# Spreading the per-token norms of the next block over the partitions: four matmuls with a broadcast column, in place of a VectorE product with the identity and one matmul with ones

## The chip, the cores and the metric

The kernel runs on one core of a Trainium2 chip. The metric is the device time of one execution in microseconds (us); of the kernel before, three runs have a median of 1286.19 us (1285.68 to 1287.00).

## The reference, cut to what matters

One layer of a streaming encoder is computed for 2048 new frames (with 16 meta tokens ahead of them) and for 32 frames of a running stream. The sums of the attention, the short convolution and the output projection stand in the kernel too; only the lines around the change are shown.

```python
def rmsnorm(x, g):
    xf = x.astype(f32)
    y = xf * lax.rsqrt(jnp.mean(xf * xf, axis=-1, keepdims=True) + EPS)
    return (y * g.astype(f32)).astype(x.dtype)
...
    q, k, v, z_a, b_g, c_g, u, z_c = split_proj(rmsnorm(hp, norm_g[l]), w_in[l])   # 1024 -> 4096 columns
...
    # attention per head: softmax(q1 k1 / 8 + bias) - lambda * softmax(q2 k2 / 8 + bias), times v
    # beside it: gated causal convolution of width 3; both are concatenated, projected, added to x, normed
```

The kernel projects x times g without its norm, and multiplies the norm of each token (one number, rsqrt of its mean square) into the results. In the projection's results the tokens lie along the free axis, so the 512 norms of a block must stand on all 128 partitions: that is the tile `rb`.

## The kernel before, in words

The 2048 frames are worked in four blocks of 512 tokens (`p` = 0 to 3; the first one carries the 16 meta tokens and the 32 sample frames as well). Within a block there are four head units `unit_a(h, p)`: projections of q, k, v and the gate z, each 24 matmuls of 512 columns (8 slices of the contraction, each as three products of high and low fp32r parts: `xh*wh`, `xl*wh`, `xh*wl`, line 225). `attend(h, p)` follows: score matmuls (L446, L447) into three buffers `s`, a minimum per row (L393, L396), an exponential (L397) which frees the score buffer, the coefficients (L370 to L377), scaling on ScalarE (L400) and combining on VectorE (L401), transposes (L462) and products with v (L469 to L471). `unit_c` computes the convolution. At the end the output projection runs in two halves (L693).

The values of v take a detour: VectorE multiplies the projection by the norms into `g` (L305), four transposes on TensorE (`ptv`, L316) turn it, and everything TensorE has behind them in its queue waits for them.

The next block is prepared during the last heads of a block. `x_stats(p + 1)` loads its rows in eight pieces `xr` (256 KB each), ScalarE squares and sums them (L115), and a short chain on VectorE and ScalarE (L117, L178 to L184) makes `r`, four norms on each partition: column t of `r` holds the norms of the 128 tokens of tile t. `x_rms(p + 1, r)` spreads `r`: VectorE multiplies the identity by each column of `r` into `dg` (four diagonal matrices side by side, L127), one fp32 matmul with `ones` as weights sums over the partitions into `pb` (L129), and ScalarE copies `pb` to `rb` (L130). `x_load(p + 1)` then loads the transposed tokens in eight pieces `xt` and splits each into `xh` (ScalarE, L152) and `xl` (VectorE, L153).

The pieces `xr`, `xt` and the product `dg` come out of one pool with the tag `xt` and eight buffers (XB = 8). `dg` is written as soon as `r` is there and is read by the matmul at the block's end, so one of the eight buffers is held for that long. Every tile of the tags `x0` to `x3` (`r` among them) and `rb` has one buffer; `pb` uses one of the two PSUM buffers `pj` of the projections.

No order is written out by hand: a scheduler puts the instructions of each engine into an order by its own estimate of time, `high_priority` moves some ahead, and each engine's queue then runs strictly in that order, SyncE's DMA issues included. So a small edit can move instructions on all engines. The transfers of weights (`wr`, 512 KB, from line 198), the loads of `xr` and `xt` and all stores are issued from SyncE's queue (the helper of line 80).

Of the kernel before, what the change touches and what calls it, by code (L numbers as in the profile page):

```python
# [11 lines left out]
F32 = mybir.dt.float32  # L12
F32R = mybir.dt.float32r
AF = mybir.ActivationFunctionType
ALU = mybir.AluOpType
AX = mybir.AxisListType

P = 128
# [9 lines left out]
QT = 512  # L28
# [7 lines left out]
XB = 8  # L36
# [11 lines left out]
def hybrid_step(ctx: ExitStack, tc: tile.TileContext, x, xT, ckT, cv, scT, rel_bias, norm_g, w_in,  # L48
# [10 lines left out]
    op = pool("op", 3)  # L59
    ap = pool("ap", 2)  # L60
    sm = pool("sm", 3)
    one = pool("one", 1)
# [6 lines left out]
    V, S, G, T = nc.vector, nc.scalar, nc.gpsimd, nc.tensor  # L69
# [16 lines left out]
    ident = const.tile([P, P], F32, name="ident")  # L86
    make_identity(nc, ident)
    ones = const.tile([P, P], F32, name="ones")
# [19 lines left out]
    def x_stats(p):  # L108

        ssq = sm.tile([P, 8], F32, tag="ssq", name="ssq", bufs=1)  # L110
        for j in range(8):
            xr = one.tile([P, QT], F32, tag="xt", name="xr", bufs=XB)
            r0 = NX + QT * p + P * (j // 2)
            dma(xr, x[r0:r0 + P, 512 * (j % 2):512 * (j % 2) + 512])
            S.activation(xr, xr, AF.Square, accum_out=ssq[:, j:j + 1])  # L115
        ssp, var, r, w = (sm.tile([P, 4], F32, tag=f"x{i}", name=f"x{i}", bufs=1) for i in range(4))
        V.tensor_reduce(ssp, ssq.rearrange("p (t i) -> p t i", i=2), op=ALU.add, axis=AX.X)  # L117
        rsqrt(r, ssp, var, w, 1.0 / D)
        return r

    def x_rms(p, r):

        rb = one.tile([P, NX + QT], F32, tag="rb", name="rb")
        pb = ps_j.tile([P, 512], F32, tag="pj", name="pb")
        dg = one.tile([P, QT], F32, tag="xt", name="dg", bufs=XB)
        with tc.high_priority():
            V.tensor_tensor(by_tile(dg), ident.unsqueeze(1).broadcast_to([P, 4, P]),  # L127
                            r.unsqueeze(2).broadcast_to([P, 4, P]), op=ALU.mult)
            T.matmul(pb, lhsT=ones, rhs=dg, start=True, stop=True)  # L129
            S.copy(rb[:, :QT], pb)  # L130
        rbs[p] = rb

# [101 lines left out]
    by_tile = lambda a: a.rearrange("p (t c) -> p t c", c=P)  # L234
# [512 lines left out]
    for p in range(NQ):  # L747
        for h in range(H):
            bz = one.tile([P, 512], F32, tag="bz", name="bz", bufs=2)
            if (h, p) != (0, 0):  # L750
                dma(bz, bzd[h])
            st = unit_a(h, p)
            if h == 2 and p < NQ - 1:
                r = x_stats(p + 1)
            if (h, p) == (0, 0):
                dma(bz, bzd[h])
            st["bz"] = bz
            if h == H - 1 and p < NQ - 1:
                x_rms(p + 1, r)
                x_load(p + 1)  # L760
            attend(h, p, st)
            if p == 0:
                attend_sample(h, st)
            for u in after[p == NQ - 1][h]:
                unit_c(u, p)
# [53 lines left out]
```

## Time and profile before

| what | value |
|---|---|
| runs, median of 3 | 1286.19 us (1285.68 to 1287.00) |
| the profiled execution's own time | 1287.04 us |
| its span | 1285.3 us |
| TensorE (PE) matmul busy | 1264.1 us, 98% of the span |
| weight loads (PEld) busy | 1099.2 us, 86% |
| VectorE (DVE) / ScalarE (ACT) / GpSimd (POOL) busy | 921.1 / 827.9 / 699.6 us |
| mean granted TensorE clock | 0.996 |

How to read it: PE, PEld, DVE, ACT, POOL and SP (SPq for its queue) are the engines; a row names the line, the operation, what it writes and reads, and in brackets how long the engine sat idle before it and what ended that. Two matmuls overlap in time, so the useful number for TensorE is the distance from start to start. L12 is line 12 of the kernel. An fp32 matmul stands as two records (two weight loads, two passes), an fp32r one as one.

### The profile page before, as it was taken

How to read it: one execution, taken by the hardware profiler on the slowest of the kernel's cores; microseconds unless marked ns; L12 is line 12 of the kernel's file. 1: busy time of each engine (PE TensorE's matmuls, PEld its weight loads, DVE VectorE, ACT ScalarE, POOL GpSimd, SP SyncE). 2: the span in 40 equal slices, each digit the busy share in tenths (PEclk: the TensorE clock that was granted, in tenths of full speed). 3: DMA queues.
4: the chain of work that ended last, by engine and by line, in shares of the span. 5: the costliest groups of instructions: out<-in, count | busy, mean ns of one | idle time of the engine just before them, and what ended most of it. 6: DMA issues, size and time to landing. Idle time of an engine off the chain costs nothing.

```text
span 1285.3 us, 21646 instructions
## 1 busy us (share of the span) xinstructions
PE 1264.1 (98%) x7058; PEld 1099.2 (86%) x7058; DVE 921.1 (72%) x2086; ACT 827.9 (64%) x2030; POOL 699.6 (54%) x918
## 2 busy tenths in 40 slices
PE   7999999999999998999999999999999999999997
PEld 6999999988888886888888888888888888888875
DVE  8667566567786847787878667767786896766663
ACT  6745454675776647677767567777777787764331
POOL 5775857767556675455465556454656483443300
PEclk9999999999999999999999999999999999999999
DMA  9744444675435447544353453344335443557752
GB/s 286 231 117 129 141 115 117 209 241 153 133 114 159 139 127 225 168 137 148 99 172 112 144 181 112 126 149 116 108 99 164 164 118 129 189 157 250 231 201 75
DMA packets 108048, 198.74 MB, mean 155 GB/s; under 512 B 17408, under 2 KB 45600, under 8 KB 107936
## 3 DMA queue, kind: packets, MB, share of 16 engines
q1 hardware_dynamic: 107936, 197.37, 49.4%
q8 instruction: 55, 0.90, 0.3%
q14 instruction: 57, 0.47, 0.1%
HBM read 145.62 MB, written 43.26 MB: 147 GB/s over the span
## 4 chain that ended last, share of the span: by engine, by line
PE 59%; DVE 1%; ACT 1%; DMA 0%; issue 0%; DVEq 0%; ACTq 0%
PE pj L225 27%; PE po L693 14%; PE s L446 4%; PE s L447 4%; PE pt L462 4%; PE po L469 2%; PE po L471 2%; PE po L470 2%; PE po L685 1%; DMA xr<-in_x 0%; PE ptv L316 0%; PE pm L474 0%; DVE p L401 0%; ACT p L397 0%; PE pss L423 0%; PE pss L424 0%
## 5 line engine op out<-in xcount | busy, mean ns | idle before, releaser
L78 POOL TENSOR_TENSOR wl<-wr,wh 128x256 fp32r<-128x256 f32 x480 | 376.8, 808 | 302.7 <-ACT wh L204 281.5
L225 PE MATMUL pj<-xh,wh 128*128 128x512 f32 (+2 forms) x1280 | 456.7, 358 | 3.2 <-DVE g L352 1.2
L225 PE MATMUL pj<-xl,wh 128*128 128x512 f32 (+2 forms) x1280 | 452.9, 354 | 1.8 <-DVE xl L153 1.8
L225 PE MATMUL pj<-xh,wl 128*128 128x512 f32 (+2 forms) x1280 | 452.4, 354 | 0.0
L225 PEld LDWEIGHTS pj<-xh,wh 128*128 128x128 f32 x1280 | 242.0, 189 | 35.2 <-issue 2.2
L225 PEld LDWEIGHTS pj<-xl,wh 128*128 128x128 f32 x1280 | 242.0, 189 | 30.7 <-DVE xl L153 2.6
L225 PEld LDWEIGHTS pj<-xh,wl 128*128 128x128 f32 x1280 | 241.6, 189 | 29.9 <-issue 0.2
L397 ACT ACTIVATE p<-s,nm 128x384 f32<-128x384 f32 (+5 forms) x352 | 208.3, 594 | 68.9 <-DVE nm L396 41.8
L204 ACT CAST wh<-wr 128x512 fp32r<-128x512 f32 x256 | 157.4, 618 | 102.5 <-PE pj L225 71.3
L401 DVE SCALAR_TENSOR_TENSOR p<-p,cf,p 128x384 f32<-128x384 f32 (+5 forms) x176 | 126.4, 747 | 24.2 <-ACT p L400 24.0
L396 DVE TENSOR_REDUCE nm<-s 128x1 f32<-128x384 f32 (+3 forms) x224 | 122.6, 560 | 22.8 <-PE s L447 22.5
L466 DVE TENSOR_TENSOR al<-pt,ah 128x512 fp32r<-128x512 f32 x144 | 97.1, 684 | 48.2 <-ACT ah L465 47.8
L78 POOL TENSOR_TENSOR cll<-ct,chh 128x256 fp32r<-128x256 f32 x80 | 64.9, 833 | 118.3 <-ACT chh L671 118.1
L446 PE MATMUL s<-ks,q 128*128 128x384 f32 (+5 forms) x352 | 127.3, 363 | 0.9 <-ACT p L397 0.8
L447 PE MATMUL s<-ks,q 128*128 128x384 f32 (+5 forms) x352 | 122.5, 349 | 0.0
L400 ACT ACTIVATE p<-p,cf 128x384 f32<-128x384 f32 (+5 forms) x176 | 99.1, 623 | 28.3 <-DVE cf L377 25.6
L465 ACT CAST ah<-pt 128x512 fp32r<-128x512 f32 x144 | 81.2, 585 | 43.0 <-PE pt L462 42.0
L393 DVE CUSTOM_DVE_ANT_0 s<-s,bz 128x512 f32<-128x512 f32 (+5 forms) x128 | 74.6, 588 | 22.0 <-PE s L447 19.7
L462 PE MATMUL pt<-ident,p 128*128 128x128 f32 x544 | 86.0, 272 | 0.0
L470 PE MATMUL po<-al,vh 128*128 128x256 f32 x288 | 82.5, 286 | 0.0
L469 PE MATMUL po<-ah,vh 128*128 128x256 f32 x288 | 81.7, 284 | 0.0
L471 PE MATMUL po<-ah,vl 128*128 128x256 f32 x288 | 81.2, 282 | 0.0
(237 smaller groups left out, 2185.4 us busy)
## 6 DMA issues: line engine op xcount, KB each, us to landing
wr<-in_w_in SPq DMA_DIRECT2D x128, 512.0 KB, 3.7
ct<-cat SPq DMA_DIRECT2D x28, 512.0 KB, 4.7
q<-q SPq DMA_DIRECT2D x64, 128.0 KB, 3.0
out<-y SPq DMA_DIRECT2D x32, 256.0 KB, 3.6
ks<-ksd SPq DMA_DIRECT2D x8, 776.0 KB, 5.0
xr<-in_x SPq DMA_DIRECT2D x24, 256.0 KB, 4.6
out<-g SPq DMA_DIRECT2D x24, 256.0 KB, 3.1
xt<-in_xT SPq DMA_DIRECT2D x24, 256.0 KB, 5.2
```

Source lines behind the costliest of these rows:

```text
L78: (engine or G).tensor_tensor(out[:, c0:c1], a[:, c0:c1], b[:, c0:c1], op=op)
L204: S.copy(wh, wi)
L225: T.matmul(ps, lhsT=a[:, k % 4], rhs=b[k][:, b0:b1], start=(k == 0 and i == 0), stop=(k == KT - 1 and i == 2))
L396: V.tensor_reduce(nm[:, c, j:j + 1], s, op=ALU.min, axis=AX.X)
L397: S.activation(pr[j][c], s, AF.Exp, bias=nm[:, c, j:j + 1], scale=-1.0, accum_out=l[:, c, j:j + 1])
L401: V.scalar_tensor_tensor(a0, a1, cf[:, 1, j:j + 1], a0, op0=ALU.mult, op1=ALU.add)
L446: T.matmul(ps, lhsT=qd[c][0][:, qs], rhs=ks[c][:, col:col + w], start=True, stop=False)
L447: T.matmul(ps, lhsT=qd[c][1][:, qs], rhs=ks[c][:, col:col + w], start=False, stop=True)
L462: T.transpose(pt[:, i, P * qi:P * (qi + 1)], cols(aa[qi], NM + P * (2 * j + i), P), ident)
L469: T.matmul(po, lhsT=vh[:, kt], rhs=ah[:, i], start=(kt == 0), stop=False)
L470: T.matmul(po, lhsT=vh[:, kt], rhs=al[:, i], start=False, stop=False)
L693: T.matmul(ps, lhsT=a[k][:, :rows], rhs=b[k], start=(k == 0 and i == 0), stop=(k == KT - 1 and i == 2))
```

## The change

The product with the identity and its buffer `dg` go. The matmul with ones becomes four matmuls of 128 columns: the weights are column t of `r`, repeated 128 times by a stride of zero, the moving operand is the identity. Each writes its quarter of `pb`.

```diff
         rb = one.tile([P, NX + QT], F32, tag="rb", name="rb")
         pb = ps_j.tile([P, 512], F32, tag="pj", name="pb")
-        dg = one.tile([P, QT], F32, tag="xt", name="dg", bufs=XB)
         with tc.high_priority():
-            V.tensor_tensor(by_tile(dg), ident.unsqueeze(1).broadcast_to([P, 4, P]),
-                            r.unsqueeze(2).broadcast_to([P, 4, P]), op=ALU.mult)
-            T.matmul(pb, lhsT=ones, rhs=dg, start=True, stop=True)
+            for t in range(4):
+                T.matmul(pb[:, P * t:P * (t + 1)], lhsT=r[:, t:t + 1].broadcast_to([P, P]), rhs=ident,
+                         start=True, stop=True)
             S.copy(rb[:, :QT], pb)
         rbs[p] = rb
```

The scheduler answers the edit with another order in many places. Three of them matter below; all lie around the end of block 1, when block 2 is loaded and the statistics of block 3 are made. Lines of the changed kernel from 129 on are one lower than in the kernel before (L305 is L304, L393 is L392, L397 is L396, L401 is L400, L446 is L445), and the numbers behind names differ by a few.

The first is VectorE's queue around the evacuation of v (L305, `g_6971`, or `g_6973` in the change), which the transposes `ptv` wait for. `cf` are the coefficients of the softmax, `s_6701` and `s_6706` (`s_6703`, `s_6708`) two score tiles of 512 columns. Before:

```order
L184 TENSOR_TENSOR x2_8734<-x2_8734,x3_8735 128x4
L376 TENSOR_TENSOR r2_6616<-r2_6616,lam2_141 128x2
L127 TENSOR_TENSOR dg_9741<-ident_100,x2_8734 128x512
L377 TENSOR_TENSOR cf_6615<-nm_6589,r2_6616 128x2x2
L393 ISA s_6701,nm_6685<-s_6701,bz_6285 128x512
L393 ISA nm_6685 128x1
L305 TENSOR_TENSOR g_6971<-pj_6984,rb_6492 128x512
```

and in the change:

```order
L183 TENSOR_TENSOR x2_8736<-x2_8736,x3_8737 128x4
L375 TENSOR_TENSOR r2_6618<-r2_6618,lam2_141 128x2
L376 TENSOR_TENSOR cf_6617<-nm_6591,r2_6618 128x2x2
L392 ISA s_6703,nm_6687<-s_6703,bz_6286 128x512
L392 ISA nm_6687 128x1
L392 ISA s_6708,nm_6687<-s_6708,bz_6286 128x512
L400 SCALAR_TENSOR_TENSOR p0_6593<-p1_6594,cf_6617,p0_6593 128x400
L400 SCALAR_TENSOR_TENSOR p0_6605<-p1_6606,cf_6617,p0_6605 128x384
L369 TENSOR_REDUCE M2_6715<-nm_6687 128x2
L304 TENSOR_TENSOR g_6973<-pj_6986,rb_6493 128x512
```

The product is gone from the queue, and a second score tile, two combining steps and a small reduction now stand ahead of the evacuation.

The second is TensorE's queue at the same place. Before:

```order
L447 MATMUL s_6706<-ks1_6342,q11_6291 128x512
L446 MATMUL s_6730<-ks0_6341,q00_6288 128x272
L447 MATMUL s_6730<-ks0_6341,q01_6289 128x272
L316 MATMUL ptv_7014<-ident_100,g_6971 128x128 x4
L225 MATMUL pj_7039<-xh0_6500,wh_7031 128x512
L225 MATMUL pj_7039<-xl0_6501,wh_7031 128x512
```

and in the change:

```order
L445 MATMUL s_6732<-ks0_6342,q00_6289 128x272
L446 MATMUL s_6732<-ks0_6342,q01_6290 128x272
L445 MATMUL s_6737<-ks1_6343,q10_6291 128x272
L446 MATMUL s_6737<-ks1_6343,q11_6292 128x272
L461 MATMUL pt_6633<-ident_100,p0_6593 128x128
...
L461 MATMUL pt_6648<-ident_100,p0_6605 128x128
L445 MATMUL s_6744<-ks0_6342,q00_6289 128x384
L446 MATMUL s_6744<-ks0_6342,q01_6290 128x384
L315 MATMUL ptv_7016<-ident_100,g_6973 128x128 x4
L224 MATMUL pj_7041<-xh0_6502,wh_7033 128x512
```

Two more pairs of score matmuls and six transposes now stand ahead of `ptv`; before, they came after it.

The third is SyncE's queue, from the last piece of block 2 to the weights of the next head (`wr_7508`, or `wr_7510` in the change). Before:

```order
L80 DMA xt_6540<-in_xT 128x512
L80 DMA vd3_135<-vl_6432 128x512
L80 DMA xr_8708<-in_x 128x512
...
L80 DMA xr_8729<-in_x 128x512
L80 DMA wr_7508<-in_w_in 128x1024
L80 DMA q00_6869<-q00_6869 64x512
```

and in the change:

```order
L80 DMA xr_8710<-in_x 128x512
L80 DMA vd3_135<-vl_6433 128x512
L80 DMA xr_8713<-in_x 128x512
...
L80 DMA xr_8731<-in_x 128x512
L80 DMA xt_9748<-in_xT 128x512
...
L80 DMA xt_9790<-in_xT 128x512
L80 DMA wr_7510<-in_w_in 128x1024
L80 DMA q00_6871<-q00_6871 64x512
```

The last piece `xt` of block 2 went far ahead, the first `xr` of block 3 has its place, and all eight `xt` of block 3 (2 MB) now stand ahead of the weights.

## Rows read from the trace of the kernel before

**Rows 1.** The page's busy times: engine, us (share of the span), instructions.

```profile
PE 1264.1 (98%) x7058; PEld 1099.2 (86%) x7058; DVE 921.1 (72%) x2086; ACT 827.9 (64%) x2030; POOL 699.6 (54%) x918
```

**Rows 2.** Who TensorE waited for, over the whole span: us in total, times, longest.

```profile
PE pv L601 <- DMA oh<-in_ohd: 3.9, 1, 3.9
PE ptv L316 <- DVE g L305: 3.4, 2, 3.2
PE pj L225 <- DVE xl L153: 1.8, 3, 1.2
PE pj L225 <- DVE g L352: 1.2, 2, 1.0
PE s L446 <- ACT p L397: 0.8, 1, 0.8
```

**Rows 3.** The tiles `pb` and `dg`: engine, line, operation, count, duration in ns (min/median/max), first and last start in us.

```profile
L129 PE MATMUL pb<-dg,ones x6: 591/592/592, 249.8 to 762.4; 128*128 128x512 f32 x6
L127 DVE TENSOR_TENSOR dg<-ident,x x3: 694/1175/1191, 59.0 to 511.9; 128x512 f32<-128x512 f32 x3
```

**Rows 4.** Weight loads in order of time, around `pb` of block 1: start us, us, row, count.

```profile
249.63 0.31 PEld L129 LDWEIGHTS pb<-dg,ones 128*128 128x128 f32 x2
250.18 0.19 PEld L446 LDWEIGHTS s<-ks,q 128*128 128x128 f32 x1 [0.24 <-issue]
250.61 0.19 PEld L447 LDWEIGHTS s<-ks,q 128*128 128x128 f32 x1 [0.24 <-issue]
```

**Rows 5.** Matmuls in order of time, around the sample's product with v, an fp32 matmul of 64 columns with 128 columns of weights (eight records in a row): start us, us, row, count.

```profile
94.53 1.00 PE L518 MATMUL pos<-o,cvt 128*128 128x64 f32 x8
95.46 0.43 PE L518 MATMUL pos<-o,cvn 48*128 48x64 f32 x2
```

**Rows 6.** TensorE in order of time, from 509.9 us on (block 1, third head).

```profile
511.21 0.40 PE L446 MATMUL s<-ks,q 128*128 128x272 f32 x1 [0.78 <-ACT p L397]
511.45 0.28 PE L447 MATMUL s<-ks,q 128*128 128x272 f32 x1
514.90 1.11 PE L316 MATMUL ptv<-ident,g 128*128 128x128 f32 x4 [3.17 <-DVE g L305]
516.24 0.63 PE L225 MATMUL pj<-xl,wh 128*128 128x512 f32 x1
516.67 0.63 PE L225 MATMUL pj<-xh,wl 128*128 128x512 f32 x1
...
520.06 0.39 PE L225 MATMUL pj<-xl,wh 128*128 128x512 f32 x1
520.29 0.39 PE L225 MATMUL pj<-xh,wl 128*128 128x512 f32 x1
...
522.14 0.82 PE L462 MATMUL pt<-ident,p 128*128 128x128 f32 x6
522.72 0.37 PE L446 MATMUL s<-ks,q 128*128 128x272 f32 x1
...
523.05 0.34 PE L446 MATMUL s<-ks,q 128*128 128x384 f32 x1
523.22 0.34 PE L447 MATMUL s<-ks,q 128*128 128x384 f32 x1
```

**Rows 7.** Stretches of the same place: from:to, length, busy us (instructions) of PE, PEld, DVE, ACT, POOL, granted TensorE clock, DMA share, GB/s.

```profile
511.30:513.20 1.90, 0.43 (x2) 0.21 (x2) 1.90 (x4) 0.00 (x0) 1.82 (x3) 1.00 0.87 240
513.20:520.00 6.80, 5.10 (x14) 4.22 (x15) 4.72 (x16) 4.15 (x11) 2.83 (x4) 0.50 1.05 363
520.00:524.00 4.00, 4.00 (x24) 3.46 (x23) 2.32 (x4) 2.96 (x6) 1.76 (x2) 1.00 0.47 182
```

**Rows 8.** VectorE in order of time: the product of block 2 at 276 us, and the place at 511 us.

```profile
276.06 1.19 DVE L127 TENSOR_TENSOR dg<-ident,x 128x512 f32<-128x512 f32 x1
...
511.86 1.18 DVE L127 TENSOR_TENSOR dg<-ident,x 128x512 f32<-128x512 f32 x1
512.96 0.68 DVE L377 TENSOR_TENSOR cf<-nm,r 128x4 f32<-128x4 f32 x1
513.56 0.69 DVE L393 CUSTOM_DVE_ANT_0 s<-s,bz 128x512 f32<-128x512 f32 x1
514.16 0.68 DVE L305 TENSOR_TENSOR g<-pj,rb 128x512 f32<-128x512 f32 x1
514.77 0.62 DVE L401 SCALAR_TENSOR_TENSOR p<-p,cf,p 128x400 f32<-128x400 f32 x1
515.31 0.69 DVE L393 CUSTOM_DVE_ANT_0 s<-s,bz 128x512 f32<-128x512 f32 x1
```

**Rows 9.** ScalarE in order of time at the same place.

```profile
509.97 0.60 ACT L204 CAST wh<-wr 128x512 fp32r<-128x512 f32 x1
...
513.67 1.13 ACT L400 ACTIVATE p<-p,cf 128x400 f32<-128x400 f32 x2 [2.51 <-DVE cf L377]
514.71 0.60 ACT L204 CAST wh<-wr 128x512 fp32r<-128x512 f32 x1
515.22 0.68 ACT L397 ACTIVATE p<-s,nm 128x512 f32<-128x512 f32 x1
```

**Rows 10.** ScalarE in order of time: the first writing of `r` for block 2 (270.86, line 179), the last piece of block 2 and the first square for block 3, and the last such square (501.79).

```profile
270.86 0.21 ACT L179 ACTIVATE x<-x 128x4 f32<-128x4 f32 x1
...
488.69 0.61 ACT L204 CAST wh<-wr 128x512 fp32r<-128x512 f32 x1
492.82 0.72 ACT L152 ACTIVATE xh<-xt,ng 128x512 fp32r<-128x512 f32 x1 [3.51 <-DMA xt<-in_xT]
494.17 0.63 ACT L115 ACTIVATE xr<-xr 128x512 f32<-128x512 f32 x1 [0.63 <-DMA xr<-in_x]
...
501.79 0.64 ACT L115 ACTIVATE xr<-xr 128x512 f32<-128x512 f32 x1
```

**Rows 11.** SyncE's DMA issues in order of time: start us, us of issuing, row, count.

```profile
486.44 0.44 SPq L80 DMA_DIRECT2D xt<-in_xT  x1
...
487.81 7.44 SPq L80 DMA_DIRECT2D xr<-in_x  x7
...
505.31 0.33 SPq L80 DMA_DIRECT2D wr<-in_w_in  x1
505.73 1.88 SPq L80 DMA_DIRECT2D q<-q  x3
```

## The prediction

> **What bounds the kernel now.** I read the page's busy times first, then TensorE's waits, then the stretches in which they lie. TensorE is the bound: matmuls cover 98% of the span, VectorE only 72% [rows 1]. The five longest waits of TensorE come to 11 us, and half of that (3.9 and 1.8) is the loading at the start [rows 2]. So an edit on VectorE gives nothing in itself; what counts is TensorE's own work and the few places where its queue stands still. The worst is at 511 us: TensorE idles 0.78 us and then 3.17 us, until VectorE's evacuation of v (L305) lets `ptv` start at 514.90 [rows 6]. [...] There a 512-column matmul starts 0.43 us after the one before (516.24 to 516.67), against 0.23 us from 520 us on (520.06 to 520.29) [rows 6]; the 5.1 us of work done there [rows 7] would have taken half, so the low clock costs 2.5 us. Idling and clock are 3.95 + 2.5 = 6.5 us, the most that can be won at one place. One of the three products `dg` lies just there, at 511.86 [rows 8].
>
> **Part 1, TensorE's own work.** Before: `pb` is two passes of 512 columns. Its neighbours' weight loads start 0.43 us apart (250.18, 250.61) [rows 4], which is the length of a pass; two are 0.86 us a block. After: four fp32 matmuls, eight loads and eight passes of 128 columns. No row has this shape. Streaming alone gives 0.43/4 = 0.107 us a pass, 0.86 us in all: the lower bound, so no gain. The nearest row is the sample's product: also 128 columns of weights to load, 64 to stream, eight records from 94.53 to 95.46, 0.116 us each [rows 5]. There the load sets the pace, not the half as long streaming. At that pace eight passes take 0.93 us, 0.07 more than before; for three blocks **+0.2 us**, all of it on the path, since TensorE is the bound. I take this value. The upper bound adds a load that nothing covers, 0.107 us for each of 24 passes: +2.6 us.
>
> The rows argue against that upper bound: the eight records of [rows 5] have 0.116 us each for load and streaming together, and half of 0.107 us of streaming laid behind a load of 0.107 would make 0.16. [...]
>
> **Part 2, VectorE's products.** Three go, 0.69 to 1.19 us each, at 59, 276 and 512 us [rows 3, 8]. At the first two no TensorE wait of [rows 2] stands behind; TensorE has other matmuls to run, so I cost them at 0. If that cover were gone, each would be worth at most its own length, 0.7 and 1.2 us. The third stands in the queue ahead of L305 and goes into part 3. `r` is now read by the matmul instead of the product, so its only buffer is held until the block's end; the next block's `r` is first written 21 us after that matmul (270.86 against 249.8 for the first) [rows 3, 10], so nothing waits.
>
> **Part 3, the stall at 511 us in the new order.** The product leaves, but other work moves ahead of L305, so I follow both queues with the distances of [rows 8]. VectorE: `cf` can start where `dg` did, 511.86, and takes 0.60; the two score tiles 0.60 each, so to 513.66; two combining steps of 0.54 (514.77 to 515.31) to 514.74; a small reduction 0.1; L305 to about 515.5. That is 0.7 later than before, although 1.1 us of work went. ScalarE: the two scalings come 0.71 after `cf` starts, so from 512.57, and take 1.04 to the next instruction; exponential 0.68, cast 0.51, exponential 0.68 end at 515.5 [rows 8, 9]. It must end before the 384-column pair can have its score buffer; that pair takes 0.35 [rows 6]. So `ptv` starts at about **515.9**, 1.0 later than 514.90. But TensorE has then done what came later before: six transposes 0.58, a 272-column pair 0.33, a 384-column pair 0.35 (522.14 to 523.40) [rows 6], 1.26 us. Net **-0.3 us**. TensorE still idles over 3 us between 511.7 and 515.9, in pieces, and I expect the clock to fall as before, at the same cost. Bounds: -6.5 if stall and clock loss both vanish, +3 if the moved work is late and the low clock lasts longer (below).
>
> **Part 4, the buffer that `dg` held.** Before, the last piece `xt` of block 2 is issued only at 486.44 and ScalarE's queue stands 3.51 us until it lands (492.82) [rows 10, 11]. In the change that piece is loaded far earlier. But now the first square for block 3 stands ahead of `xh7` in ScalarE's queue, and its `xr` takes the place in SyncE's queue that the piece had. So the same wait is due, by another transfer. After it ScalarE is ahead by one square, 0.63 us. VectorE is busy without a break before L305, so I cost this at **0**; the bound is 3.5 us earlier on ScalarE, which is rival A. The eight `xt` of block 3 ahead of the weights cost 0 as long as they are through when the weights are asked for at 505.31 [rows 11].
>
> **Sum.** +0.2 - 0.3 = -0.1 us. On the profiled execution's own 1287.04 us that is 1286.9; that one lay 0.85 over the median of the runs, and on the median 1286.19 it is **1286.1 us**. No change can be told from a difference below 0.2%, 2.6 us.
>
> **Rivals.** *A, the stall shrinks and the clock stays.* With the awaited piece loaded and a product less, ScalarE and VectorE come to 511 us earlier. For it: 3.51 us of waiting [rows 10] and 1.18 us of product [rows 8] lie ahead of a 3.17 us stall. Against it: the new order puts a square ahead of `xh7`, and more ahead of L305. If the idling drops by about 1.5 us and the granted clock stays at 1.00, it gives 1.5 + 2.5 = 4 us: 1282.2 us, at the most 1279.7. Chance 0.28.
>
> *B, the weights come late.* In SyncE's queue eight `xt`, 2 MB, now stand ahead of `wr_7510`, each waiting for a square to free its buffer. Weights issued at 505.31 [rows 11] and before are cast on ScalarE at 510 to 515, in front of exponentials that TensorE waits for [rows 9]. At 363 GB/s, what the transfers reach in [rows 7], 2 MB take 5.8 us. As the squares end at 502 [rows 10], they fit, just. The point that decides is whether the weights land after about 511: then ScalarE's queue stands up to 3 us at the cast, the stall grows by that, and a longer low clock adds some 1 us: 1290 us. Against it: the pieces leave the crowded stretch after 513 us, where the DMA share is 1.05 [rows 7]. Chance 0.20.
>
> *C, the loads are not covered.* Part 1's upper bound, +2.6 - 0.3: 1288.5 us. Chance 0.04, since [rows 5] speak against it.
>
> **How the numbers follow.** The forecast has 0.48: between 1284 and 1288, for the small moves elsewhere, where the remaining waits of [rows 2] are about 1 us. Faster by over 0.2% is A, 0.28 and a little of the forecast's edge, 0.29. Slower is B and most of C, 0.23. Within 0.2%: 0.48. The range leaves out the far end of A (below 1281.5) and of B (above 1290.0): 1281.5 to 1290.0. Signs are spread, so the forecast's own range, 1284 to 1288, is the narrower statement.
>
> **What would show it.** Right: `pb` as eight records about 0.11 us apart, no L127, `ptv` of block 1's third stall starting some 1 us of TensorE work later than before, a stretch of granted clock 0.50 again near 513 to 520 us. A is right if that stretch is gone and no idling over 2 us stands there. B is right if ScalarE's cast there waits for a DMA of `wr`. C is right if `pb` takes 1.7 us. I am wrong altogether if a new wait of TensorE over 1 us stands where [rows 2] have none, or if the time moves without any change in its waits.

## The result, and the profile after

The changed kernel is slower: 1289.15 us median of 19 runs (1286.70 to 1291.68) against 1286.40 us of the kernel before (19 runs on the same chip, 1285.45 to 1287.64), a ratio of 1.0021 with a 95% interval of 1.0015 to 1.0028. The forecast was no change, between 1284 and 1288 us. The runs of the changed kernel lie 5 us apart, those of the kernel before 2.2 us.

The profiled execution took 1287.71 us (span 1285.9), so it is one of the better ones of the changed kernel, while the profiled execution of the kernel before (1287.04) was one of its worse. Page against page shows almost nothing [rows 1]:

```profile
PE 1263.4 (98%) x7076; PEld 1098.5 (85%) x7076; DVE 919.7 (72%) x2083; ACT 827.5 (64%) x2030; POOL 688.9 (54%) x918
```

Who TensorE waited for in the changed kernel (us in total, times, longest), against [rows 2]:

```profile
PE pv L600 <- DMA oh<-in_ohd: 4.0, 1, 4.0
PE s L445 <- ACT p L396: 2.8, 2, 2.6
PE pj L224 <- DVE xl L152: 2.0, 3, 1.1
PE pt L461 <- DVE p L400: 1.7, 2, 1.4
PE pj L224 <- DVE g L351: 1.2, 2, 1.0
PE ptv L315 <- DVE g L304: 1.2, 2, 0.8
```

Three things stand in it. The wait of 3.2 us for the evacuation of v is gone, and a wait of 2.6 us for an exponential has its place. A wait of 1.4 us of `pt` is new; [rows 2] have none like it. And `ptv` still waits 0.8 us, but elsewhere (at 657 us, where it waited 0.24 before).

The four matmuls of `pb` for block 1, TensorE in order of time (start us, us, row, count); in the kernel before, the pair took 0.86 us [rows 3, 4]:

```profile
249.29 1.06 PE L127 MATMUL pb<-ident,x 128*128 128x128 f32 x8
250.10 0.31 PE L445 MATMUL s<-ks,q 128*128 128x144 f32 x1
```

From the first pass to the next instruction's start it is 0.81 us.

The place at 511 us in the changed kernel, TensorE, against [rows 6]:

```profile
511.68 0.28 PE L446 MATMUL s<-ks,q 128*128 128x272 f32 x1
514.56 0.39 PE L445 MATMUL s<-ks,q 128*128 128x272 f32 x1 [2.59 <-ACT p L396]
514.79 0.29 PE L446 MATMUL s<-ks,q 128*128 128x272 f32 x1
514.91 0.81 PE L461 MATMUL pt<-ident,p 128*128 128x128 f32 x6
515.74 0.45 PE L445 MATMUL s<-ks,q 128*128 128x384 f32 x1
...
516.20 0.60 PE L315 MATMUL ptv<-ident,g 128*128 128x128 f32 x4
```

and VectorE there, against [rows 8]:

```profile
512.09 0.58 DVE L376 TENSOR_TENSOR cf<-nm,r 128x4 f32<-128x4 f32 x1
...
515.08 0.67 DVE L304 TENSOR_TENSOR g<-pj,rb 128x512 f32<-128x512 f32 x1
```

`cf` starts nearly where the product stood before, L304 starts 0.9 us later than before, `ptv` 1.3 us later, and TensorE has done two pairs and six transposes first. The stretch of [rows 7] (from:to, length, busy us of PE, PEld, DVE, ACT, POOL, granted clock, DMA share, GB/s) now reads:

```profile
513.20:520.00 6.80, 5.43 (x29) 4.55 (x30) 5.87 (x20) 6.16 (x19) 2.35 (x4) 1.00 0.52 164
```

The clock stayed at 1.00 after an idling of 2.6 us, where [rows 7] have 0.50. In this stretch the changed kernel wins against this profile of the kernel before, and TensorE starts `ptv` at 657.52 us, 1.5 us earlier than there. It loses most of that again at 854 us, in block 2 (the `ptv` that follows there starts at 855.14 against 855.72). TensorE there:

```profile
852.77 0.40 PE L446 MATMUL s<-ks,q 128*128 128x512 f32 x1
854.54 0.77 PE L461 MATMUL pt<-ident,p 128*128 128x128 f32 x5 [1.37 <-DVE p L400]
```

and VectorE at the same time:

```profile
852.98 0.17 DVE L376 TENSOR_TENSOR cf<-nm,r 128x8 f32<-128x8 f32 x1
853.07 0.57 DVE L395 TENSOR_REDUCE nm<-s 128x1 f32<-128x400 f32 x1
853.85 0.63 DVE L400 SCALAR_TENSOR_TENSOR p<-p,cf,p 128x400 f32<-128x400 f32 x1 [0.21 <-ACT p L399]
```

Nothing of the change is near: five transposes stand in TensorE's queue at a time when the coefficients of their softmax (`cf`) are only just made.

### The profile page after: what moved, and what is told of

Read it like the earlier page. It is cut to its first block, busy times and chain, and to the rows that moved or that the text cites. A ratio compares the mean times of both kernels' runs of the same rounds, so it can differ in the third digit from the quotient of the medians.

```text
span 1285.9 us, 21685 instructions
## 1 busy us (share of the span) xinstructions
PE 1263.4 (98%) x7076; PEld 1098.5 (85%) x7076; DVE 919.7 (72%) x2083; ACT 827.5 (64%) x2030; POOL 688.9 (54%) x918
## 4 chain that ended last, share of the span: by engine, by line
PE 56%; DVE 3%; ACT 2%; issue 1%; DMA 0%; SPq 0%; DVEq 0%; ACTq 0%
PE pj L224 25%; PE po L692 13%; PE s L445 4%; PE s L446 3%; PE pt L461 3%; PE po L469 2%; PE po L470 2%; PE po L468 2%; DVE p L400 1%; PE po L684 1%; DMA out<-y 0%; ACT p L396 0%; PE ptv L315 0%; ACT xr L115 0%; PE pm L473 0%
## 5 line engine op out<-in xcount | busy, mean ns | idle before, releaser
L78 POOL TENSOR_TENSOR wl<-wr,wh 128x256 fp32r<-128x256 f32 x480 | 372.5, 799 | 307.9 <-ACT wh L203 295.7
L396 ACT ACTIVATE p<-s,nm 128x384 f32<-128x384 f32 (+5 forms) x352 | 208.2, 594 | 70.5 <-DVE nm L395 45.7
L400 DVE SCALAR_TENSOR_TENSOR p<-p,cf,p 128x384 f32<-128x384 f32 (+5 forms) x176 | 123.3, 730 | 21.6 <-ACT p L399 21.1
L445 PE MATMUL s<-ks,q 128*128 128x384 f32 (+5 forms) x352 | 127.1, 363 | 3.0 <-ACT p L396 2.8
L446 PE MATMUL s<-ks,q 128*128 128x384 f32 (+5 forms) x352 | 122.9, 350 | 0.0
L392 DVE CUSTOM_DVE_ANT_0 s<-s,bz 128x512 f32<-128x512 f32 (+5 forms) x128 | 74.1, 587 | 21.1 <-PE s L446 14.7
```

Source lines behind the costliest of these rows:

```text
L78: (engine or G).tensor_tensor(out[:, c0:c1], a[:, c0:c1], b[:, c0:c1], op=op)
L396: S.activation(pr[j][c], s, AF.Exp, bias=nm[:, c, j:j + 1], scale=-1.0, accum_out=l[:, c, j:j + 1])
L400: V.scalar_tensor_tensor(a0, a1, cf[:, 1, j:j + 1], a0, op0=ALU.mult, op1=ALU.add)
L445: T.matmul(ps, lhsT=qd[c][0][:, qs], rhs=ks[c][:, col:col + w], start=True, stop=False)
L446: T.matmul(ps, lhsT=qd[c][1][:, qs], rhs=ks[c][:, col:col + w], start=False, stop=True)
```

## The experiments

The scheduler's part had to be separated from the work's. So most kernels here hold the order: before the program is closed, each engine's instructions are chained in a recorded order (the added edges fix the order of issue alone), and the scheduler can't move them. Chaining and the four matmuls together cost nothing measurable: `keep_product` below has both, and the time of the kernel before.

```diff
+def in_order(tc):
+    a = np.cumsum(np.frombuffer(zlib.decompress(base64.b85decode(ORDER)), dtype=np.int16).astype(np.int64))
...
+        seq = [mine[e][k] for k in a[at:at + len(mine[e])]]
+        for i, j in zip(seq, seq[1:]):
+            tc.add_manual_dep(j, i.name, mybir.DependencyInfo(mybir.DependencyClass.NoSync, mybir.DependencyReason.DATA),
+                              reason="in_order")
...
         hybrid_step(tc, *args)
+        in_order(tc)
```

`ORDER` holds, for each engine, the numbers of its instructions as they are written in the program, in the order wanted. Against the kernel before, the changed kernel's own order moves 1301 of TensorE's 7016 other instructions and some 420 each of VectorE's 1955 and ScalarE's 1612. All engines change order together in these runs; which engine's order costs what is not separated. The two orders come together again between the blocks, so a kernel can follow one up to a point and the other from there. Theory "order": the loss lies in the places of instructions that have nothing to do with `pb`. Rival "work": the matmuls with a broadcast column, or the buffer, cost it. The runs were made on several chips, each beside runs of the kernel before on the same chip. So kernels are compared by their ratios to it, and a difference in us below is a difference of such ratios, at 1286.4 us; the medians are as measured.

**The changed kernel again** (no edit).

> The changed kernel a second time, for a second profiled execution and more runs. Both theories: 1289.2 us, between 1286.7 and 1291.7. Its runs lie 5 us apart where those of the kernel before lie 2.2 apart, so this look may be at another kind of execution: if the 2.6 us stall at 514 us sometimes lets the granted clock fall as the 3.2 us stall of the kernel before did, this profile can show 0.50 somewhere in 513 to 522 us, and a time some 2 to 4 us above an execution that shows 1.00 there.

1288.64 us, ratio 1.0021 (1.0013 to 1.0030). The same loss. The profile shows the waits again (`s` 2.7 us at 514 us, `pt` 1.4 us, `ptv` 0.8 us), but the clock did fall this time, for half of the stretch:

```profile
513.20:520.00 6.80, 5.44 (x24) 4.96 (x25) 6.03 (x20) 5.76 (x17) 2.37 (x4) 0.75 0.47 143
```

The low clock is 0.50 from 514.07 to 517.48 us; in the first profile that window has 1.00. So whether a low clock followed an idling of 2.6 to 2.7 us differed between these two executions; at some 1.7 us (half of 3.4 us, my estimate) it may be part of the 5 us between runs. The new waits at 262 and 270 us also differ (0.3 and under 0.2 us here, under 0.2 and 0.2 in the first profile).

**The change's work in the old order.** Edit: `in_order` with the order of the kernel before, the four matmuls where the one stood.

> The changed work (four matmuls in each of three blocks, no product, no buffer for it) with every engine's instructions held in the order of the kernel before; the four matmuls stand where the one stood. Theory 'order' (the planner laid the queues out anew, and the loss lies in that layout, not in the work): 1286.4, within 0.6 of the kernel before, with the stall of 3.2 us at 511 us and the clock at 0.50 for some 7 us behind it as in rows 2 and 7. Rival 'work' (the matmuls with a broadcast column as weights, or the buffer that dg no longer takes, cost it): 1289.2, as the changed kernel.

1284.76 us, ratio 0.9987 (0.9978 to 0.9996): *faster* than the kernel before by 1.7 us. "Work" has fallen, and "order" must account for 4.4 us, not 2.7; that the work would win something, neither theory had expected. What it wins stands at 511 us. Who TensorE waited for:

```profile
PE ptv L315 <- DVE g L304: 2.3, 2, 2.0
...
PE pj L224 <- DVE M L373: 0.6, 1, 0.6
PE s L445 <- ACT p L396: 0.5, 1, 0.5
```

VectorE there, now without the product of [rows 8]:

```profile
511.47 0.57 DVE L183 TENSOR_TENSOR x<-x,x 128x4 f32<-128x4 f32 x1
511.97 0.15 DVE L375 TENSOR_TENSOR r<-r,lam 128x2 f32<-128x2 f32 x1
512.15 0.58 DVE L376 TENSOR_TENSOR cf<-nm,r 128x4 f32<-128x4 f32 x1
512.65 0.69 DVE L392 CUSTOM_DVE_ANT_0 s<-s,bz 128x512 f32<-128x512 f32 x1
...
513.26 0.68 DVE L304 TENSOR_TENSOR g<-pj,rb 128x512 f32<-128x512 f32 x1
```

The wait of 3.2 us is 2.0 us, shorter by what the product took. The clock fell for half of the stretch of [rows 7], 3.4 us in place of 6.8 (0.50 from 514.07 to 517.48 us):

```profile
513.20:520.00 6.80, 6.00 (x21) 4.96 (x22) 4.51 (x15) 5.00 (x14) 2.91 (x5) 0.75 1.03 369
```

**Only the matmuls.** Edit, on top of the kernel above:

```diff
+        dg = one.tile([P, QT], F32, tag="xt", name="dg", bufs=XB)
         with tc.high_priority():
+            V.tensor_tensor(by_tile(dg), ident.unsqueeze(1).broadcast_to([P, 4, P]),
+                            r.unsqueeze(2).broadcast_to([P, 4, P]), op=ALU.mult)
             for t in range(4):
```

> The four matmuls, in the order of the kernel before, but VectorE's product and its buffer are kept (nothing reads the product any more). Between this and the kernel before lies TensorE's work alone; between this and old_order lie the product and the buffer alone. Theory 'the product stood in the queue': the 1.4 us by which old_order beats the kernel before come from the third product (1.18 us at 511.86 in rows 8), which VectorE no longer has ahead of L305: this run gives 1286.1, within 0.5, with the wait of ptv at 3.2 us again (old_order: 2.0). Rival 'the matmuls are cheaper': 1284.8, as old_order, with the wait at 2.0.

1286.87 us, ratio 1.0003 (0.9995 to 1.0012): as the kernel before. TensorE's waits and VectorE's queue are those of before, too:

```profile
PE ptv L318 <- DVE g L307: 3.1, 2, 2.9
...
PE s L448 <- ACT p L399: 1.1, 1, 1.1
```

```profile
513.38 1.18 DVE L127 TENSOR_TENSOR dg<-ident,x 128x512 f32<-128x512 f32 x1
514.48 0.68 DVE L379 TENSOR_TENSOR cf<-nm,r 128x4 f32<-128x4 f32 x1
...
515.69 0.68 DVE L307 TENSOR_TENSOR g<-pj,rb 128x512 f32<-128x512 f32 x1
```

So the four matmuls cost nothing that can be measured (the interval is -0.6 to +1.5 us), and removing the products is worth 1.0003 - 0.9987, 2.1 us. (As nobody reads these products, their buffers are free after the write; the buffer alone is not separated here.)

**Four times the matmuls, old order.** Edit:

```diff
-            for t in range(4):
+            for t in [0, 1, 2, 3] * 4:
```

> As the run before, but the four matmuls issued four times over (16 in place of 4 in each of three blocks: 24 more passes a block, 72 in all; the result is the same). Theory 'order': the passes cost what lies between their starts in the profile of the changed kernel, 0.112 us each: 72 x 0.112 = 8.1, so 1294.5, and without any new wait. Rival 'work': a pass costs more than that, above all if the load ahead of each is not covered (0.19 us more, 72 x 0.30 = 21.7): over 1300.

1288.29 us, ratio 1.0017 (1.0009 to 1.0026), 3.9 us above `old_order` and not 8.1. The passes cost what was expected. TensorE in block 2's preparation:

```profile
489.91 3.73 PE L127 MATMUL pb<-ident,x 128*128 128x128 f32 x32
493.40 0.48 PE L224 MATMUL pj<-xh,wl 128*128 128x512 f32 x1
```

3.49 us, where `old_order` has 0.81; so 2.68 us a block and 8.0 in all. The other 4.1 us were won back in TensorE's waits and by the clock. TensorE came later here and waited less for the other engines: in this run's profile `ptv` waits 1.2 us in place of 2.0, the wait of 1.0 us for L351 at 490 us and that of 0.5 us for L396 are gone, and there is no low clock (1.00 from 513.2 to 520 us, where `old_order` has 0.75; some 1.7 us, half of 3.4, an estimate); together 4.0 us. I had overlooked that.

**One stretch of the new order at a time.** Edit: `ORDER` is the old order, but the changed kernel's in one stretch.

> The changed work in the order of the kernel before, except for the first 188 us, where every engine follows the changed kernel's order (34 of TensorE's instructions move). Theory 'the order of each stretch has its own price': the distances between TensorE's starts from 80 to 100 us show 2.4 us above the bare passes in old_order and 1.2 in the changed kernel, so this stretch is worth -1.2: 1284.8 - 1.2 = 1283.6. Rival 'the stretches do not add up' (what is won early is waited away at 511 us, where TensorE waits for VectorE): 1284.8, with a wait at 511 us that is 1.2 longer.

> The changed work in the old order, except from 188 to 473 us, where every engine follows the changed kernel's order (251 of TensorE's instructions move). Theory 'each stretch has its own price', from the distances between TensorE's starts in two profiles of the changed kernel against old_order: +1.1 to +2.1 at 260 to 280 us and +0.5 at 320 to 340 us, so 1284.8 + 2.1 = 1286.9. Rival 'what is lost early is given back at the wait at 511 us, which ends at a fixed time': 1284.8, with that wait shorter than in old_order.

> The changed work in the order of the kernel before, except between 473 and 690 us, where every engine follows the order of the changed kernel. Theory 'order', with the share of each stretch read from the two profiles: in this stretch the new order is the better one by 3.2 us (the stall at 511 us is 2.6 in place of 3.2 + 0.8 and the clock stays at 1.00), so 1286.4 - 3.2 = 1283.2, faster than both kernels; some 1285.5 if the clock falls behind the 2.6 us stall in most executions. Rival 'work': 1289.2 or above.

> The changed work in the old order, except from 690 to 875 us (119 of TensorE's instructions move). This stretch holds the new wait of 1.4 us at 854 us, where six transposes stand in TensorE's queue ahead of the coefficients they need. Theory: +1.5, so 1286.3, with 'pt L461 waits for p L400, 1.4' among TensorE's waits. Rival: the wait comes from what happened before 690 us and is not there in this run: 1284.8.

> The changed work in the old order up to 875 us and in the changed kernel's order from there (568 of TensorE's instructions move). The two profiles of the changed kernel show almost no longer distances there than old_order (0.6 at 1190 us in one, 0 in the other): 1285.0, between 1284.6 and 1285.6. With this run all five stretches have been tried one at a time (60 to 188: -2; 473 to 690: +1.4). Theory 'they add up': -2 + 2.1 + 1.4 + 1.5 + 0.2 = +3.2 above old_order, 1288.0, against 1288.6 to 1289.2 measured for the changed kernel. If this run is over 1286, the profiles hide something after 875 us.

| stretch in the new order | median, us | ratio to before (95%) | against `old_order`, us |
|---|---|---|---|
| none (`old_order`) | 1284.76 | 0.9987 (0.9978 to 0.9996) | |
| 60 to 188 us | 1282.67 | 0.9972 (0.9961 to 0.9982) | -1.9 |
| 188 to 473 us | 1287.11 | 1.0007 (0.9998 to 1.0016) | +2.6 |
| 473 to 690 us | 1286.13 | 0.9998 (0.9989 to 1.0007) | +1.4 |
| 690 to 875 us | 1286.15 | 0.9998 (0.9989 to 1.0007) | +1.4 |
| 875 us to the end | 1285.92 | 0.9994 (0.9985 to 1.0003) | +0.9 |

They add up to +4.4 us; with the 1.7 us of the work that is +2.7, and the changed kernel has +2.7 (ratio 1.0021). Each value alone is uncertain by more than 1 us, so the agreement is better than it has to be. The first, the largest and the sign of the sum are clear; +1.4, +1.4 and +0.9 can't each be told from nothing by the times, and rest on the waits that the profiles show.

The profiles name the places. With the new order from 60 to 188 us the wait of 0.6 us behind `M` (above, `old_order`) is gone, and in this run's profile the clock does not fall at 514 us (1.00 from 513.2 to 520 us). From 188 to 473 us TensorE gets through less in the same time; at 330 us its queue has (compare 328.48 and 328.61 in `old_order`, without a wait):

```profile
329.54 0.29 PE L446 MATMUL s<-ks,q 128*128 128x272 f32 x1
330.20 0.66 PE L315 MATMUL ptv<-ident,g 128*128 128x128 f32 x4 [0.37 <-DVE g L304]
```

The rest of the 2.6 us there is in gaps under 0.2 us, mostly from 260 to 282 us; I can't put it on single instructions. It is not the clock, which averaged 0.75 from 513.2 to 520 us in this run's profile as in that of `old_order`. From 473 to 690 us TensorE's waits are

```profile
PE s L445 <- ACT p L396: 3.0, 2, 2.6
...
PE ptv L315 <- DVE g L304: 0.8, 1, 0.8
```

so I had this stretch with the wrong sign in its expectation: I had compared the profile of the kernel before, with a low clock for all of 6.8 us (0.50), with one of the changed kernel that had none (1.00); this run's has 0.75. From 690 to 875 us the wait at 854 us is there, though all before it runs in the old order:

```profile
PE pt L461 <- DVE p L400: 1.4, 1, 1.4
```

and from 875 us on, two waits at 1190 us that I had not listed, behind a VectorE that idles 1.6 us for ScalarE (L480):

```profile
PE pss L422 <- DVE sqh L419: 0.5, 1, 0.5
PE pss L423 <- DVE sqh L420: 0.4, 1, 0.4
```

**One instruction moved.** Edit: in `old_order`'s table, VectorE's L304 goes ahead of L181, past eight instructions; nothing else moves on any engine.

> old_order with one single instruction moved: the evacuation of v (L304) that ptv waits for at 511 us goes ahead of eight small VectorE instructions (the norms of block 3, which nobody reads before 760 us, the coefficients and a score tile), from 513.26 to about 510.5. Theory 'TensorE waits for nothing but this queue': ptv starts when TensorE comes to it, the wait of 2.0 us goes, the clock does not fall (another 1.7), and what then comes 0.6 later on VectorE (cf) is not waited for: 1284.8 - 3.7 = 1281.1. Rival 'another wait takes its place' (cf is late, so are the transposes of p and the score buffers): 1283 to 1285.

1281.55 us, ratio 0.9962 (0.9949 to 0.9974), 3.2 us below `old_order`. VectorE:

```profile
510.25 0.68 DVE L304 TENSOR_TENSOR g<-pj,rb 128x512 f32<-128x512 f32 x1
...
512.55 0.71 DVE L376 TENSOR_TENSOR cf<-nm,r 128x4 f32<-128x4 f32 x1
```

TensorE:

```profile
511.37 0.29 PE L446 MATMUL s<-ks,q 128*128 128x272 f32 x1
511.49 0.60 PE L315 MATMUL ptv<-ident,g 128*128 128x128 f32 x4
511.85 0.48 PE L224 MATMUL pj<-xh,wh 128*128 128x512 f32 x1
```

The stretch of [rows 7]:

```profile
513.20:520.00 6.80, 6.80 (x36) 5.78 (x35) 5.40 (x15) 5.13 (x14) 3.93 (x6) 1.00 1.06 384
```

Wait and low clock are gone (1.00, where `old_order` has 0.75), and `cf` comes 0.4 us later without anyone on TensorE waiting. In `old_order` the projection of v that L304 reads was finished by 510.4 us (its last matmul there: 509.90, 0.48 us long), yet L304 started at 513.26, behind eight instructions of which three make norms for 760 us. It started 0.61 us after the last of them (512.65), and in `v_first`, ahead of them, at 510.25.

**Both of the good ones.** Edit: the new order to 188 us, the old one from there, and L304 moved.

> Both: the changed kernel's order for the first 188 us, the old one from there, and the evacuation of v moved as in v_first. If the two add up: 1284.8 - 1.2 - 3.7 = 1279.9, faster than either kernel by 0.5%. If TensorE only arrives earlier at a wait that ends at a fixed time: as v_first, 1281.1.

1280.47 us (1279.50 to 1280.82), ratio 0.9951 (0.9939 to 0.9964). It beats the kernel before by 6.3 us and the changed kernel by some 9. They don't add up in full: 0.9962 to 0.9951 is 1.4 us, not 1.9, and the intervals overlap.

**The buffer alone, in the scheduler's own order.** Edit on the kernel before:

```diff
-        dg = one.tile([P, QT], F32, tag="xt", name="dg", bufs=XB)
+        dg = rb[:, :QT]
```

> The kernel before, with product and single matmul as they were, and one edit: the product is written into the columns of rb that the copy fills afterwards, so it takes no buffer of the eight. The scheduler orders this kernel by itself. It moves 1610 of TensorE's 7016 instructions, against 1301 for the change under study, for an edit that takes no work away. Theory 'an edit draws a new order, and the order decides': any time from 1283 to 1290, more than 0.7 from 1286.4, explained by waits of TensorE that the kernel before does not have or no longer has. Rival 'the order is worth little, this change's was an odd case': 1286.4, within 0.7.

1297.56 us, ratio 1.0090 (1.0076 to 1.0103). This does not test what it was meant to. `rb` has one buffer, so the product can't be written before the last reader of the old norms is through, and TensorE waits for it in each block:

```profile
PE pb L129 <- DVE rb L127: 7.1, 3, 3.8
```

That is a new dependence, not an order. It tells nothing of the orders' worth, and what the buffer of `dg` costs stays open.

**Two more orders for known work.** Work whose time in the old order is measured, now left to the scheduler.

> The work of keep_product (four matmuls, the product kept and read by nobody), in the order that the scheduler makes of it by itself: 723 of TensorE's instructions stand otherwise than in the kernel before. keep_product, the same work in the old order, has 1286.9. Theory 'a new order has no reason to be as good, and the old one happens to be good': slower, 1287.5 to 1291, by waits of TensorE that keep_product doesn't have. Rival 'the order draws either way': as likely faster, 1283 to 1286.5. Rival 'the loss was special to the changed kernel': within 0.7 of 1286.9.

1289.85 us, ratio 1.0019 (1.0010 to 1.0028); in the old order 1.0003, so the scheduler's order costs 2.1 us. Its waits hold the one of the changed kernel at 854 us again:

```profile
PE ptv L318 <- DVE g L307: 3.1, 2, 2.8
PE pt L464 <- DVE p L403: 1.4, 1, 1.4
```

> The work of old_order_x4 (the four matmuls issued four times over), in the order that the scheduler makes of it by itself: 1444 of TensorE's instructions stand otherwise than in the kernel before, 1140 otherwise than in the changed kernel. The same work in the old order has 1288.3. Theory: slower, 1289 to 1293. Rival 'either way': 1284 to 1288. Rival 'special to the changed kernel': within 0.7 of 1288.3.

1295.11 us, ratio 1.0067 (1.0054 to 1.0079), slower than the theory's range; in the old order 1.0017, so 6.4 us. Its waits:

```profile
PE s L445 <- ACT p L396: 4.1, 2, 3.2
...
PE pt L461 <- DVE pt L456: 1.0, 1, 1.0
```

With the changed kernel (1.0021 against 0.9987, 4.4 us) that is three kinds of work, and each time the order newly made is the worse one. It is not a rule that it must be: the first 188 us of the new order are better by 1.9 us. But the order that the kernel before had is a good one of those that this scheduler made here, and each edit that was left to it moved hundreds of TensorE's instructions (1301, 723 and 1444).

## Why the prediction was wrong

**The step that failed is the sum.** It has two terms, +0.2 for the matmuls and -0.3 for the place at 511 us, and says that "the small moves elsewhere" are covered by a range of 1284 to 1288. So the rest of the new order stands in the sum at nothing, without a reason. It was 972 of the 1301 moves on TensorE, and it cost -1.9 + 2.6 + 1.4 + 0.9 = +3.0 us. (The whole order costs 4.4 us and the stretch around 511 us 1.4, which leaves the same 3.0.) Of this the 1.4 us from 690 to 875 us match the new wait at 854 us; most of the 2.6 us from 188 to 473 us can't be put on instructions. I had the order of the changed kernel for all of the program, but followed it only where the trace of before shows a long wait. A new order can make a wait where there was none: the one at 854 us is over 1 us and has nothing like it in [rows 2], which is what the prediction itself had named as the sign that it was wrong altogether.

**Part 1** was right in that the matmuls cost next to nothing. Eight passes take 0.81 us against 0.86, the forecast's lower bound and not its pace of 0.116 us a pass; the term of +0.2 is within what can be measured (`keep_product`, 1.0003). Rival C is out: its time, 1288.5 us, came near the measured one by chance, but `pb` takes 0.81 us and not the 1.7 it needed. The 0.107 us that it put for an uncovered load was my estimate: no run shows such a load. A load is 0.19 us long [rows 4], and the eight of `pb` are through in 0.98 us (from 249.17), beside the passes. In `old_order_x4` 32 loads and passes of 128 columns take 3.49 us, 0.109 us each, 0.002 more than the 0.107 that was put for streaming alone (0.43/4, an estimate), so the loads are covered. That streaming alone does not set the pace in [rows 5] fits what stands beside `pb`: passes of 144 columns start 0.10 to 0.12 us apart (250.25, 250.37, 250.47, 250.59 in the changed kernel), hardly less than with 272 (0.12 to 0.13: 248.54, 248.67, 248.79). That the load sets it was my reading; the loads ahead of the 144 columns start 0.11 us apart (250.08, 250.19, 250.30).

**Part 2**: the first two products were worth nothing that a run shows apart. Removing the three is worth 2.1 us, which the profiles put at the third, and the prediction lost sight of it. It put that product into part 3, where other work takes its place in the new order, and so never asked what the removal wins when the order stays. That was the largest single effect of the change itself, and it has the other sign.

**Part 3** was right for its stretch in the path that it followed: `ptv` forecast at 515.9 and measured at 516.20. L304 was forecast from 514.84 (its 515.5 is the end) and started at 515.08, because `cf` started 0.23 us late. TensorE idled 2.6 us in one piece; the forecast's own terms leave 4.2 - 1.26 = 2.9 us in pieces, not "over 3". The clock was forecast to fall as before; it stayed up in one profile of the changed kernel (1.00 from 513.2 to 520 us) and fell for half as long in the other (0.75). The forecast was -0.3 us, and the run with only this stretch in the new order has 0.9998 of the time before, -0.3 us. That the tenths agree is luck: the interval there is over 1 us either way, the 1.7 us that the work wins and the 1.4 us that this part of the order costs nearly cancel in it, and the clock was not as forecast.

**Part 4** was right in that the wait changed hands: ScalarE's queue in the changed kernel idles 2.52 us before the first square (493.49; its `xr`, issued at 487.19, landed 6.2 us later, at 493.40), where it idled 3.51 us before the last piece [rows 10].

**Rival A** came true by half: in the first profile the clock stayed at 1.00, but an idling of 2.59 us stands there, where its sign asked for none over 2 us. Its gain of 4 us did not come, and in the second profile the clock fell too (0.75). **Rival B** did not happen: in the profile after, ScalarE has no wait for a `wr` transfer between 494 and 512 us. The forecast's chance of 0.23 for "slower" stood on B and C, and neither had a part in it: the mechanism that made it slower was not among the rivals.

A second fault is in the base. I costed the low clock at 2.5 us from one execution, in which it was 0.50 for all of 513.2 to 520.0 us [rows 7]. That execution had 1287.04 us where the median is 1286.4; in fourteen other profiles taken here the mean clock of this stretch is 1.00 in seven, 0.75 in five, and 0.64 and 0.61 in the other two (`keep_product`, in the old order and in its own). What can be won at 511 us is shown by `v_first`: 3.2 us beyond the product.

## What to carry to other kernels

Where a scheduler sets the order, an edit has two prices, that of its work and that of the new order, and they are measured apart by holding the old order for the new work; here they were -1.7 and +4.4 us. In a forecast, go through the *whole* new queue of the engine that is the bound, and look at each place where an instruction now stands sooner after the one that feeds it; waits in the old trace only show where the old order was bad. (That such a reading would have found the 3.0 us here is not shown.) And when one engine idles behind another's queue, see whether what it waits for was ready long before: moving one such instruction won more than the edit could.

## What the runs showed of the hardware that had not been expected

The granted clock after one and the same idling was not the same in each execution. Behind 2.6 to 2.7 us of idling at 514 us it stayed at 1.00 in one profile of the changed kernel and averaged 0.75 over 513.2 to 520 us in the next; behind 2.0 us it averaged 0.75 in `old_order` and 1.00 in the run with the new order to 188 us. By my estimate the two profiles of the changed kernel differ by 1.7 us for it (half of 3.4 us at 0.50), and one profile alone can't price such a wait closer than that.
